# Both halves of the activations in one 512-column product, scaled and shifted ahead of it, and one adaLN vector from VectorE to TensorE

## The chip, the cores and the metric

The kernel runs on one core of one Trainium2 chip. The metric is device microseconds of one execution, weights and activations coming from HBM in float32 and the output going back to it. Three runs of the kernel before gave 672.47 us as their median (672.23 to 672.62).

## The reference

A trunk of two layers on a sequence of 256 tokens with 1024 channels. Layer 0 mixes tokens with a causal convolution module, layer 1 with causal attention of 16 heads; each mixer is followed by an MLP of 4096 hidden units with a squared ReLU. Six vectors per layer (shift, scale and gate of the mixer, then of the MLP) come from a conditioning vector `c` by a product with `ada_w`, called adaLN here.

```python
cond = silu(c)
for i in range(2):
    sh1, sc1, g1, sh2, sc2, g2 = split(cond @ ada_w[i] + ada_b[i], 6)
    h = rms_norm(x, mix_norm_g[i]) * (1 + sc1) + sh1
    y = conformer_conv(h, ...) if i == 0 else attention(h, w_qkv, q_norm_g, k_norm_g, w_o)
    x = x + g1 * y
    h = rms_norm(x, mlp_norm_g[i]) * (1 + sc2) + sh2
    x = x + g2 * (square(relu(h @ mlp_w1[i])) @ mlp_w2[i])
```

Everything is float32. The result must come out at nearly float32 accuracy.

## The kernel before

Activations lie transposed: 8 tiles (`KT`) of 128 channels by 256 tokens (`S`). `xT` holds the residual stream. A large product is done in float32r, a format with a shorter mantissa, and regains its accuracy by splitting: an operand is a high half plus a low half. For weights, `split` (lines 191 to 202) has ScalarE cast a loaded block `raw` of 128 x 2048 to the high half `wh` (L196), in two pieces of 1024 columns in the calls that matter here, and VectorE subtract to get the low half `wl` (L199; in layer 0 a quarter of it, 256 columns of each piece, goes to GpSimd, L201). For activations the halves are `xh` and `xl`, for the MLP's hidden values `sh` and `sl`, for attention's output `oh` and `ol`. `mm3` (lines 207 to 211) then makes one step of k, that is 128 input channels, out of three products: high weights on the high activations, high weights on the low ones, low weights on the high ones.

The normalization is put off. `norm_prep` (from L718) multiplies `xT` by the scale vector alone (`gm`) and splits it. The factor of each token, one over the root mean square, is not known yet when the first products start: `norm_scale` makes it during them, has it spread over the partitions as `rs_ext` (its copy there is called the seam), and `evict` (L796 and L797) multiplies each finished tile by it on VectorE. The shift vector rides along as two more columns of the activations, so these products have `NE` = 258 columns, and the bias that results stands in column 256 of the evicted tile and is added by the next operation on ScalarE.

An MLP (`mlp`, from L820) has two loops. **w1**: the 32 tiles `f` of 128 hidden units are made from 16 weight blocks of 256 units, two tiles a block, 8 steps of k a tile. `six` does the first three blocks in an order of its own, since the token factors come during them; the loop from L845 does blocks 3 to 15. Each tile goes through `finish` (L829 to 836): eviction (L797), Relu with its bias on ScalarE (L833), the square twice, once cast to the high half (L834, L835), and the low half by a subtraction on VectorE (L836). **w2**: from L868, four blocks of two output tiles, 32 steps of k each; a finished tile is scaled by the gate and added to `xT` by one VectorE operation (L881).

Attention makes q, k and v from twelve blocks of `w_qkv`, three for each `b` of 0 to 3 (q, k and v of four heads, `z` = 0, 1, 2; loop from L1049, `take` evicting with L797), and works on one group of heads while the products of the next run. Of that work the change touches `squares` (adds the biases to q and k, L951) and `values` (adds it to v); `norms` takes one over the root of the heads' mean squares with `rsqrt` (L175 to L180, eleven small VectorE operations, each waiting for the last) and widens it by a copy to `rb` (L971), which TensorE then transposes (`kb`, L991). `kouter` (from L763) is the output projection of both mixers.

TensorE's order is the order in which the code is written: `tick` counts steps of k, and `at(d, f)` puts `f` behind `d` more steps. The other engines' instructions are ordered by a scheduler, which weighs when their inputs should be ready. Loads are issued by SyncE in the order of its queue, into five buffers called `raw`.

adaLN vectors are made in two ways. `ada_dve` (L289) loads a quarter of a vector's weights (1 MB) and has VectorE multiply and add it in four pieces (L299, L301); after the last quarter `colsum` (L263) sums over partitions on TensorE (`cs`, L267) and two more small products turn the sum. `ada_pe` makes the same quarter with `gemv4` (L248): TensorE products on float32, each set of four side by side with 32 columns of weights. In the first MLP six vectors go the VectorE way: `slots` says after which block of w1 or w2 each quarter comes.

## Time and profile before

| | before |
|---|---|
| median of three runs | 672.47 us (672.23 to 672.62) |
| the profiled execution | 670.39 us |
| its span, first to last instruction | 668.6 us |
| TensorE products / weight loads, busy | 654.0 us / 605.2 us |
| VectorE, ScalarE, GpSimd, busy | 494.2, 369.2, 125.6 us |
| moved by DMA | 150.07 MB, 224 GB/s on average |
| conv layer | up to 155.98 us |
| first MLP, w1 and w2 | 155.98 to 253.5, 253.5 to 350.3 us |
| attention | 350.3 to 476.9 us |
| second MLP, w1 and w2 | 476.9 to 571.1, 571.1 to 664.1 us |

How to read it. PE is TensorE's products, PEld its weight loads, which overlap them; DVE is VectorE, ACT ScalarE, POOL GpSimd, SP SyncE. A product's length in a row is the time from its start to its modelled end, which overlaps the next, so the pace is read from the distance of starts, or from the number of products in a stretch. A row of windows has the stretch, its length, then for PE, PEld, DVE, ACT and POOL the busy time with the number of instructions in brackets, then TensorE's granted clock (1.00 is 2.4 GHz, 0.50 is 1.2 GHz), the busy share of the 16 DMA engines, and GB/s; where only one tile's or line's instructions are asked for, engines that have none are left out. A row of a timeline has the start, the length, engine, line, operation, output and inputs, sizes, the number of instructions put together, and in brackets the idle time before it with what ended it.

### The profile page before, as it was taken

What the parts mean: (1) busy time and instruction counts of PE and PEld (TensorE: products, weight loads), DVE (VectorE), ACT (ScalarE), POOL (GpSimd) and SP (SyncE); (2) the same over time, 40 slices, a digit from 0 to 9 for tenths busy, and PEclk for the clock granted to TensorE, in tenths of its full rate; (3) what the DMA queues carried; (4) which work ended last, traced back from release to release, by engine and by line L of the source; (5) the groups of instructions that cost most, each with busy time, mean ns of one, the idle gap of its engine ahead of it and who ended that gap; (6) DMA issues with size and microseconds to landing.
All of it is one profiled execution on the core that took longest, in us unless ns stands there. A gap on an engine that the chain in (4) does not pass through costs nothing.

```text
span 668.6 us, 14398 instructions
## 1 busy us (share of the span) xinstructions
PE 654.0 (98%) x5909; PEld 605.2 (91%) x5909; DVE 494.2 (74%) x924; ACT 369.2 (55%) x678; POOL 125.6 (19%) x167
## 2 busy tenths in 40 slices
...
GB/s 302 340 351 295 240 2 373 216 251 211 151 250 336 346 278 349 342 349 336 349 337 130 237 97 112 181 123 105 101 169 205 334 293 191 186 188 178 110 17 17
DMA packets 107871, 150.07 MB, mean 224 GB/s; under 512 B 2871, under 2 KB 91120, under 8 KB 107806
## 3 DMA queue, kind: packets, MB, share of 16 engines
...
q14 instruction: 19, 0.16, 0.1%
...
q10 hardware_dynamic: 144, 0.06, 0.0%
...
## 4 chain that ended last, share of the span: by engine, by line
PE 68%; DVE 21%; issue 4%; ACT 3%; POOL 2%; DMA 2%; SPq 1%; DVEq 0%; ACTq 0%; POOLq 0%
PE m L208 11%; PE m L210 11%; PE m L209 11%; DVE ada_a L301 8%; DVE wl L199 7%; PE qkv L208 4%; PE qkv L209 3%; PE qkv L210 3%; PE cv L403 3%; PE ko L209 2%; PE ko L208 2%; PE ci L208 2%; PE ko L210 2%; PE rep L393 2%; PE ci L210 2%
## 5 line engine op out<-in xcount | busy, mean ns | idle before, releaser
L199 DVE TENSOR_TENSOR wl<-raw,wh 128x1024 fp32r<-128x1024 f32 (+2 forms) x176 | 204.5, 1181 | 59.0 <-ACT wh L196 57.8
L196 ACT CAST wh<-raw 128x1024 fp32r<-128x1024 f32 x176 | 177.7, 1043 | 107.0 <-PE m L209 58.8
L210 PE MATMUL m<-xh,wl 128*128 128x258 f32 x512 | 144.5, 282 | 1.2 <-DVE wl L199 1.1
L208 PE MATMUL m<-sh,wh 128*128 128x256 f32 x512 | 145.4, 284 | 0.0
L210 PE MATMUL m<-sh,wl 128*128 128x256 f32 x512 | 144.3, 282 | 0.8 <-DVE wl L199 0.8
L208 PE MATMUL m<-xh,wh 128*128 128x258 f32 x512 | 145.1, 283 | 0.0
L209 PE MATMUL m<-xl,wh 128*128 128x258 f32 x512 | 144.7, 283 | 0.0
L209 PE MATMUL m<-sl,wh 128*128 128x256 f32 x512 | 144.0, 281 | 0.0
L210 PEld LDWEIGHTS m<-xh,wl 128*128 128x128 f32 x512 | 96.7, 189 | 1.8 <-DVE wl L199 1.8
L208 PEld LDWEIGHTS m<-sh,wh 128*128 128x128 f32 x512 | 96.4, 188 | 1.6 <-issue 0.8
L210 PEld LDWEIGHTS m<-sh,wl 128*128 128x128 f32 x512 | 96.4, 188 | 1.2 <-DVE wl L199 1.2
L208 PEld LDWEIGHTS m<-xh,wh 128*128 128x128 f32 x512 | 96.5, 188 | 1.0 <-issue 0.4
L209 PEld LDWEIGHTS m<-xl,wh 128*128 128x128 f32 x512 | 96.8, 189 | 0.0
L209 PEld LDWEIGHTS m<-sl,wh 128*128 128x128 f32 x512 | 96.4, 188 | 0.0
L201 POOL TENSOR_TENSOR wl<-raw,wh 128x256 fp32r<-128x256 f32 (+1 forms) x60 | 67.7, 1141 | 105.4 <-ACT wh L196 90.7
L301 DVE SCALAR_TENSOR_TENSOR ada_a<-raw,cond,ada_a 128x512 f32<-128x512 f32 x98 | 81.9, 867 | 0.9 <-DMA raw<-in_ada_w_dram 0.7
L208 PE MATMUL qkv<-xh,wh 128*128 128x258 f32 x192 | 56.4, 294 | 0.0
L209 PE MATMUL qkv<-xl,wh 128*128 128x258 f32 x192 | 54.2, 282 | 0.0
L210 PE MATMUL qkv<-xh,wl 128*128 128x258 f32 x192 | 54.1, 282 | 0.0
L833 ACT ACTIVATE s<-tx 128x256 f32<-128x256 f32 x64 | 31.8, 506 | 36.8 <-DVE tx L797 36.7
L730 POOL TENSOR_TENSOR acc<-acc,nsq 128x256 f32<-128x256 f32 x15 | 14.1, 937 | 155.4 <-ACT nsq L728 154.9
L208 PEld LDWEIGHTS qkv<-xh,wh 128*128 128x128 f32 x192 | 36.2, 189 | 4.2 <-issue 4.2
(256 smaller groups left out, 1125.2 us busy)
## 6 DMA issues: line engine op xcount, KB each, us to landing
...
```

The lines of the kernel that those rows point to most:

```text
L196: box["cut"] = [act.copy(wh[:, a:a + n], r[:, a:a + n]).ins]
L199: box["cut"].append(dve.tensor_sub(wl[:, a:m], r[:, a:m], wh[:, a:m].bitcast(F32)).ins)
L201: pool.tensor_tensor(wl[:, m:a + n], r[:, m:a + n], wh[:, m:a + n].bitcast(F32), op=OP.subtract)
L208: pe.matmul(ps, wh, ah, start=start, stop=False, **kw)
L209: pe.matmul(ps, wh, al, start=False, stop=False, **kw)
L210: pe.matmul(ps, wl, ah, start=False, stop=stop, **kw)
L301: dve.scalar_tensor_tensor(a, w, cond[:, k, 0:1], a, op0=OP.mult, op1=OP.add)
L393: pe.matmul(ps[32 * r:32 * r + 32, :284], ident[:, 32 * g:32 * g + 32], UT[i][:, r:r + 284], start=True, stop=True, tile_position=(0, 32 * ...
L403: pe.matmul(ps[32 * g:32 * g + 32, :S], W[:, g, q, :], G[:, g, 4 * q:4 * q + S], start=(q == 0), stop=(q == 7), tile_position=(0, 32 * g))
L730: pool.tensor_tensor(acc, acc, q, op=OP.add)
L833: act.activation(s, t[:, :S], AF.Relu, bias=t[:, S:S + 1])
```

## The change

Five things are changed. `xh` and `xl` become the two halves of one tile `X[0]` (named `xa`), beside each other for each k, and a second such tile `X[1]` (`xb`) is made after the conv layer. A new `mm2` does one step of k with two products where `mm3` has three: the high weights on both halves at once, 512 columns, into the two halves of one PSUM bank, and the low weights on the high half, 256 columns, into the first. It is used in w2 of both layers (512 steps), in blocks 5 to 15 of w1 of layer 1 (`MERGED`, 176 steps), and in seven of the twelve qkv blocks, from `b` = 1, `z` = 2 on (112 steps).

The bias columns fall away there: `whole` makes activations that are fully normalized, scaled and shifted: `xT` times `rs_ext` on VectorE, the same Identity with scale and bias twice on ScalarE (once cast to the high half), a subtraction on VectorE. It runs for the eight tiles at blocks 3 and 4 of w1 in both layers, into `xb`, and at `b` = 1, `z` = 0 and 1 of qkv, into `xa`. From block 5 on w1 reads `xb`. Layer 0 keeps `mm3` there, with 256 columns, and its Relu reads PSUM directly. Where `mm2` was used, the two halves of the bank are added: by `join` (a copy of one half on ScalarE, an addition on VectorE) in w1 and qkv, and in w2 by a second operation on `xT` like the first. In layer 1's shifted tiles VectorE makes the squared Relu, ScalarE the cast.

`su` now stores 24 of the 32 hidden tiles with both halves, the other eight go into `X[0]`, and `oh` and `ol` are the halves of `X[1]`. Tiles of q, k and v are used where they were evicted; only tiles that were not shifted still get their bias there.

The adaLN vector (1, 3), the shift of layer 1's MLP, leaves the first MLP, where VectorE made it in 16 pieces, and is made by TensorE at four qkv blocks (`ADA_AT`); the slots of the other five are spaced anew.

```diff
+MERGED = (1,)
+ADA_AT = ((1, 1), (1, 2), (2, 1), (2, 2))
...
+    def mm2(ps, wh, wl, a, start, stop):
+        pe.matmul(ps.rearrange("p (a s) -> p a s", a=2), wh, a, start=start, stop=False, skip_group_check=True)
+        pe.matmul(ps[:, :S], wl, a[:, 0, :], start=False, stop=stop, skip_group_check=True)
+        tick()
...
+    def whole(l, m, i, n):
+        t = work.tile([P, S], F32, name="nsq")
+        dve.tensor_mul(t, xT[:, i, :], rs_ext[:, :S])
+        g, b = gm[:, l, m, i:i + 1], mod[:, l, 3 * m, i:i + 1]
+        act.activation(X[n][:, i, 0, :S], t, AF.Identity, bias=b, scale=g)
+        act.activation(t, t, AF.Identity, bias=b, scale=g)
+        dve.tensor_sub(X[n][:, i, 1, :S], t, X[n][:, i, 0, :S].bitcast(F32))
+
+    def join(ps, t):
+        act.copy(t, ps[:, S:])
+        box["evict"] = dve.tensor_tensor(t, ps[:, :S], t, op=OP.add).ins
...
-            def finish(ps, f):
+            def both(f):
+                n = FF // P - KT
+                return su[:, f] if f < n else X[0][:, f - n, :, :S]
+
+            def finish(ps, f, shifted=False):
                 t = mp.tile([P, NE], F32, name="tx", bufs=3)
-                evict(ps, t)
                 s = mp.tile([P, S], F32, name="s2", bufs=4)
-                act.activation(s, t[:, :S], AF.Relu, bias=t[:, S:S + 1])
-                act.activation(sh[:, f, :], s, AF.Square)
-                act.activation(s, s, AF.Square)
-                dve.tensor_sub(sl[:, f, :], s, sh[:, f, :].bitcast(F32))
+                if shifted:
+                    if l in MERGED:
+                        join(ps, t[:, :S])
+                    if l not in MERGED:
+                        act.activation(s, ps[:, :S], AF.Relu)
+                    elif l == 0:
+                        act.activation(s, t[:, :S], AF.Relu)
+                    else:
+                        dve.scalar_tensor_tensor(s, t[:, :S], 0.0, t[:, :S], op0=OP.max, op1=OP.mult)
+                else:
+                    evict(ps, t)
+                    act.activation(s, t[:, :S], AF.Relu, bias=t[:, S:S + 1])
+                u = both(f)
+                if shifted and l == 1:
+                    act.copy(u[:, 0, :], s)
+                else:
+                    act.activation(u[:, 0, :], s, AF.Square)
+                    act.activation(s, s, AF.Square)
+                dve.tensor_sub(u[:, 1, :], s, u[:, 0, :].bitcast(F32))
...
             for b in range(3, FF // 256):
                 with tc.issue_after(box["seam"]) if b > 3 else ExitStack():
                     wh, wl = w1_split(b)
+                if b in (3, 4):
+                    for i in range(4 * b - 12, 4 * b - 8):
+                        whole(l, 1, i, 1)
+                if b == 5:
+                    use(1)
...
+                        if b > 4 and l in MERGED:
+                            mm2(ps, wh[:, o:o + P], wl[:, o:o + P], X[1][:, k, :, :S], k == 0, k == KT - 1)
+                        else:
+                            n = NE if b < 5 else S
+                            mm3(ps[:, :n], wh[:, o:o + P], wl[:, o:o + P], xh[:, k, :n], xl[:, k, :n],
+                                start=(k == 0), stop=(k == KT - 1))
+                    finish(ps, f, b > 4)
...
-                            mm3(ps[j][:, :S], wh[:, o:o + P], wl[:, o:o + P], sh[:, kk, :], sl[:, kk, :],
-                                start=(kk == 0), stop=(kk == FF // P - 1))
+                            mm2(ps[j], wh[:, o:o + P], wl[:, o:o + P], both(kk), kk == 0, kk == FF // P - 1)
...
-                        dve.scalar_tensor_tensor(xT[:, n, :], ps[j][:, :S], mod[:, l, 5, n:n + 1],
-                                                 xT[:, n, :], op0=OP.mult, op1=OP.add)
+                        for h in range(2):
+                            dve.scalar_tensor_tensor(xT[:, n, :], ps[j][:, h * S:h * S + S], mod[:, l, 5, n:n + 1],
+                                                     xT[:, n, :], op0=OP.mult, op1=OP.add)
...
-    seq = [[(0, 5), (1, 1)], [(1, 0), (1, 2), (1, 4), (1, 3)]]
+    seq = [[(0, 5), (1, 1)], [(1, 0), (1, 2), (1, 4)]]
...
-            slots[3 + n * 12 // len(fs) if half == 0 else 15 + n * 15 // len(fs)].append(f)
+            slots[5 + n * 9 // len(fs) if half == 0 else 14 + n * 16 // len(fs)].append(f)
...
+                if (b, z) in ADA_AT:
+                    kp = ADA_AT.index((b, z))
+                    r = ada_load(1, 3, kp)
+                    at(15, lambda kp=kp, r=r: fin3.append(ada_pe(1, 3, kp, r)))
+                    if kp == 3:
+                        at(20, lambda: fin3[3]())
...
+                if b == 1 and z < 2:
+                    for i in range(4 * z, 4 * z + 4):
+                        whole(1, 0, i, 0)
```

In the two qkv loops `mm3` and `evict` become `mm2` and `join` for the seven blocks named above (a tile made so counts as `shifted`).

How the order of instructions moves is shown at three places; in these rows a name's number tells one buffer from another, and a line number is that of the kernel the row is from. The first is ScalarE in w1 of layer 0, around the cast of block 5's weights. Before (`wh_2405` is block 5; `s2_2279` and `s2_2311` are tiles 6 and 7):

```order
L835 ACTIVATE s2_2230<-s2_2230 128x256
L835 ACTIVATE s2_2237<-s2_2237 128x256
L833 ACTIVATE s2_2279<-tx_2277 128x256
L196 CAST wh_2405<-raw_2403 128x1024
L834 ACTIVATE sh_1997<-s2_2279 128x256
L833 ACTIVATE s2_2311<-tx_2309 128x256
L835 ACTIVATE s2_2279<-s2_2279 128x256
L834 ACTIVATE sh_1997<-s2_2311 128x256
L196 CAST wh_2405<-raw_2403 128x1024
```

After (`wh_2434` is block 5; `xb_1995` and the `nsq` tiles belong to `whole`, `s2_2394` and `s2_2426` to tiles 8 and 9):

```order
L815 ACTIVATE xb_1995<-nsq_2358,mod_142,gm_143 128x256
L876 ACTIVATE s2_2394<-tx_2393 128x256
L816 ACTIVATE nsq_2358<-nsq_2358,mod_142,gm_143 128x256
L815 ACTIVATE xb_1995<-nsq_2363,mod_142,gm_143 128x256
L881 ACTIVATE su_2000<-s2_2394 128x256
L816 ACTIVATE nsq_2363<-nsq_2363,mod_142,gm_143 128x256
L882 ACTIVATE s2_2394<-s2_2394 128x256
L876 ACTIVATE s2_2426<-tx_2425 128x256
L202 CAST wh_2434<-raw_2432 128x1024
L881 ACTIVATE su_2000<-s2_2426 128x256
L202 CAST wh_2434<-raw_2432 128x1024
```

Between the last operation of tiles 0 to 5 and that cast now stand 26 operations instead of one: 16 of `whole` and 10 of `finish` for tiles 6 to 9. In layer 1 there are 28.

The second place is VectorE at the same point, up to the low half of block 5. Before (`wl_2406` is that low half, `tx_2309` tile 7's eviction, `ada_a` the accumulation of an adaLN quarter):

```order
L797 TENSOR_TENSOR tx_2309<-m1_2284,rs_ext_142 128x258
L299 TENSOR_SCALAR ada_a_2318<-raw_2316,cond_104 128x512 x2
L301 SCALAR_TENSOR_TENSOR ada_a_2318<-raw_2316,cond_104,ada_a_2318 128x512
L836 TENSOR_TENSOR sl_1998<-s2_2279,sh_1997 128x256
L301 SCALAR_TENSOR_TENSOR ada_a_2318<-raw_2316,cond_104,ada_a_2318 128x512
L199 TENSOR_TENSOR wl_2406<-raw_2403,wh_2405 128x768
L836 TENSOR_TENSOR sl_1998<-s2_2311,sh_1997 128x256
L797 TENSOR_TENSOR tx_2358<-m1_2333,rs_ext_142 128x258
L199 TENSOR_TENSOR wl_2406<-raw_2403,wh_2405 128x768
```

After (`wl_2435` is that low half, `tx_2425` tile 9's eviction, the subtractions into `xb` and the `nsq` product are of `whole`, the one into `su` is tile 8's):

```order
L824 TENSOR_TENSOR tx_2425<-m1_2400,rs_ext_140 128x258
L311 TENSOR_SCALAR ada_a_2506<-raw_2504,cond_104 128x512 x2
L817 TENSOR_TENSOR xb_1995<-nsq_2348,xb_1995 128x256
L817 TENSOR_TENSOR xb_1995<-nsq_2353,xb_1995 128x256
L813 TENSOR_TENSOR nsq_2363<-xT_137,rs_ext_140 128x256
L313 SCALAR_TENSOR_TENSOR ada_a_2506<-raw_2504,cond_104,ada_a_2506 128x512 x2
L817 TENSOR_TENSOR xb_1995<-nsq_2358,xb_1995 128x256
L313 SCALAR_TENSOR_TENSOR ada_a_2506<-raw_2583,cond_104,ada_a_2506 128x512
L817 TENSOR_TENSOR xb_1995<-nsq_2363,xb_1995 128x256
L883 TENSOR_TENSOR su_2000<-s2_2394,su_2000 128x256
L313 SCALAR_TENSOR_TENSOR ada_a_2506<-raw_2583,cond_104,ada_a_2506 128x512 x2
L205 TENSOR_TENSOR wl_2435<-raw_2432,wh_2434 128x768 x2
```

The low half now comes behind the eviction of tile 9, seven pieces of adaLN and six short operations, where it came behind tile 7's.

The third place is VectorE in attention, where `norms` of the first group of heads ends in `rb`. Before:

```order
L179 SCALAR_TENSOR_TENSOR rsq_t_4727<-rsq_t_4727,vs_4724 128x16
L951 TENSOR_SCALAR q_4894<-tqkv_4757 128x256
L180 SCALAR_TENSOR_TENSOR rsq_y_4726<-rsq_t_4727,rsq_y_4726 128x16
L178 TENSOR_TENSOR rsq_t_4727<-rsq_y_4726 128x16
L199 TENSOR_TENSOR wl_4979<-raw_4976,wh_4978 128x1024
L179 SCALAR_TENSOR_TENSOR rsq_t_4727<-rsq_t_4727,vs_4724 128x16
L199 TENSOR_TENSOR wl_4979<-raw_4976,wh_4978 128x1024
L180 SCALAR_TENSOR_TENSOR rsq_y_4726<-rsq_t_4727,rsq_y_4726 128x16
L797 TENSOR_TENSOR tqkv_4792<-qkv_4767,rs_ext_142 128x258
L971 COPY rb_4740<-rsq_y_4726 128x512
L974 TENSOR_TENSOR ws_4742<-vs_4724,rsq_y_4726 128x8
```

After (`tk_4564` is an eviction of the second group; L1011 adds a bias; `xa` and `nsq` are of `whole`):

```order
L185 SCALAR_TENSOR_TENSOR rsq_t_4477<-rsq_t_4477,vs_4474 128x16
L817 TENSOR_TENSOR xa_138<-nsq_4524,xa_138 128x256
L186 SCALAR_TENSOR_TENSOR rsq_y_4476<-rsq_t_4477,rsq_y_4476 128x16
L824 TENSOR_TENSOR tk_4564<-qkv_4539,rs_ext_140 128x258
L184 TENSOR_TENSOR rsq_t_4477<-rsq_y_4476 128x16
L1011 TENSOR_SCALAR tq_4456<-tq_4456 128x256
L185 SCALAR_TENSOR_TENSOR rsq_t_4477<-rsq_t_4477,vs_4474 128x16
L1011 TENSOR_SCALAR tq_4507<-tq_4507 128x256
L186 SCALAR_TENSOR_TENSOR rsq_y_4476<-rsq_t_4477,rsq_y_4476 128x16
L817 TENSOR_TENSOR xa_138<-nsq_4529,xa_138 128x256
L1031 COPY rb_4490<-rsq_y_4476 128x512
L1034 TENSOR_TENSOR ws_4492<-vs_4474,rsq_y_4476 128x8
```

Between `vs`, with which `norms` begins, and `rb` now stand eight short operations of `whole` and one piece of a weight block's low half, where two such pieces stood.

## Rows read from the trace of the kernel before

**Rows 1.** Engines (page, part 1): busy us (share of the span) and instructions
```profile
PE 654.0 (98%) x5909; PEld 605.2 (91%) x5909; DVE 494.2 (74%) x924; ACT 369.2 (55%) x678; POOL 125.6 (19%) x167
```

**Rows 2.** Stages (windows): w1, w2 of layer 0; attention; w1 of layer 1
```profile
156.00:253.50 97.50, 96.30 (x805) 94.40 (x803) 90.29 (x152) 67.23 (x127) 31.10 (x32) 1.00 0.78 260
253.50:350.30 96.80, 95.97 (x816) 93.78 (x814) 91.93 (x118) 44.05 (x64) 41.01 (x35) 1.00 1.02 345
350.30:476.90 126.60, 125.24 (x1043) 114.00 (x1043) 100.91 (x278) 75.70 (x165) 3.43 (x23) 1.00 0.45 144
476.90:571.10 94.20, 94.20 (x793) 93.66 (x793) 75.38 (x130) 70.42 (x134) 2.10 (x3) 1.00 0.66 216
```

**Rows 3.** Waits of TensorE: us in total, times, longest
```profile
PE m L210 <- DVE wl L199: 1.8, 3, 0.8
```

**Rows 4.** Windows of the products alone: w1, then w2, of layer 1
```profile
510.10:561.70 51.60, 51.60 (x434) 51.60 (x433) 7.55 (x18) 0.00 (x0) 1.00 0.87 288
577.20:594.30 17.10, 17.10 (x146) 17.10 (x145) 0.48 (x1) 0.00 (x0) 1.00 0.56 181
```

**Rows 5.** Timeline of TensorE, an adaLN product in the conv stage: start, us
```profile
106.73 1.91 PE L248 MATMUL ada<-raw,cond 128*32 128x256 f32 x32
108.46 0.40 PE L403 MATMUL cv<-xg,W 128*32 128x256 f32 x4
```

**Rows 6.** Timeline of TensorE, a column sum
```profile
350.26 0.64 PE L267 MATMUL cs<-ada_a,ones 128*32 128x256 f32 x8
```

**Rows 7.** Timeline of ScalarE, first tiles of w1 in layer 0, then layer 1
```profile
174.36 0.91 ACT L833 ACTIVATE s<-tx 128x256 f32<-128x256 f32 x2 [2.04 <-DVE tx L797]
180.47 0.50 ACT L833 ACTIVATE s<-tx 128x256 f32<-128x256 f32 x1
180.87 1.04 ACT L196 CAST wh<-raw 128x1024 fp32r<-128x1024 f32 x1
...
495.03 0.91 ACT L833 ACTIVATE s<-tx 128x256 f32<-128x256 f32 x2 [1.95 <-DVE tx L797]
501.13 0.50 ACT L833 ACTIVATE s<-tx 128x256 f32<-128x256 f32 x1
```

**Rows 8.** Line 443: durations min/median/max in ns, first and last start
```profile
L443 ACT ACTIVATE h<-xg,mod,gm x8: 583/592/602, 45.4 to 59.5; 128x256 f32<-128x256 f32 x8
```

**Rows 9.** Timeline of VectorE, w1 of layer 0
```profile
173.91 1.82 DVE L797 TENSOR_TENSOR tx<-m,rs_ext 128x258 f32<-128x258 f32 x5
175.65 0.95 DVE L199 TENSOR_TENSOR wl<-raw,wh 128x768 fp32r<-128x768 f32 x1
...
189.50 1.40 DVE L301 SCALAR_TENSOR_TENSOR ada_a<-raw,cond,ada_a 128x512 f32<-128x512 f32 x2
190.82 0.41 DVE L836 TENSOR_TENSOR sl<-s,sh 128x256 fp32r<-128x256 f32 x1
```

**Rows 10.** Windows of the w1 products alone, up to block 5, layers 0, 1
```profile
155.90:186.40 30.50, 29.33 (x240) 28.89 (x241) 3.48 (x9) 0.00 (x0) 1.00 0.45 145
476.90:507.20 30.30, 29.14 (x240) 28.87 (x241) 3.52 (x9) 0.00 (x0) 1.00 0.35 108
```

**Rows 11.** Windows at the program's end; timeline of TensorE at its start
```profile
665.20:667.20 2.00, 0.00 (x0) 0.00 (x0) 0.00 (x0) 0.37 (x1) 0.00 (x0) 1.00 0.43 131
667.30:668.50 1.20, 0.00 (x0) 0.00 (x0) 0.00 (x0) 0.00 (x0) 0.00 (x0) 0.50 0.00 0
...
2.63 3.78 PE L117 MATMUL wu<-ident 128*128 128x128 f32 x16
12.81 1.60 PE L117 MATMUL wu<-ident 128*128 128x128 f32 x12
```

**Rows 12.** Timelines of VectorE and of TensorE in attention
```profile
381.10 0.41 DVE L971 COPY rb<-rsq_y 128x512 f32<-128x512 f32 x1
...
382.06 0.60 PE L991 MATMUL kb<-ident,rb 128*128 128x128 f32 x4
```

**Rows 13.** Timeline of VectorE at the program's end
```profile
664.18 0.48 DVE L881 SCALAR_TENSOR_TENSOR xT<-m,mod,xT 128x256 f32<-128x256 f32 x1 [2.36 <-PE m L210]
```

60 lines of the change are left out of this document (38 added, 22 removed).

## The prediction

> **What bounds the kernel now.** The busy share comes first: TensorE is busy for 98% of the span [rows 1]. In the view of the stages it stays so in both MLPs and in attention, and the only other thing that is full anywhere is in the first MLP, where VectorE is busy for 90.29 of 97.5 us in w1 and 91.93 of 96.8 us in w2, with the DMA engines at 1.02 in w2 [rows 2]. The view of waits asks whether these hold TensorE up: hardly, for in both MLPs it waited only three times, 1.8 us in all, for the low half of a weight [rows 3]. So the time is the pace of TensorE's products, and that pace is the next thing to read: 144 products of w2 of the second MLP in 17.1 us, and 432 of its w1 in 51.6 us (the counts shown have two more that reach over an edge) [rows 4]. That is 119 ns each, 356 and 358 ns for the three that make one step of k; qkv has w1's 258 columns, and I give it w1's pace.
>
> **The product of 512 columns.** A step was three products of 256 columns and becomes one of 512 and one of 256. This holds for 512 steps of w2 (256 per layer), 176 of w1 (blocks 5 to 15 of layer 1) and 112 of qkv (seven of twelve weight blocks): 800 steps. No row shows a float32r product of 512 columns. The nearest is adaLN's float32 product: eight sets of four side by side took 1.73 us from 106.73 to 108.46 [rows 5], 216 ns a set, where a set of 256 float32 columns keeps the array nearly twice as long as 256 float32r columns do. The bounds around it: a step stays at 356 ns if 512 columns cost twice 119, and it falls to 216 + 108 = 324 ns if the 256-column product too ran at half of that set. Between them stands the case that the 12 ns by which 119 exceeds 256 columns at 2.4 GHz (106.7 ns; the granted clock is 1.00 [rows 4]) are paid once per product: 225 + 119 = 344 ns. I take 216 + 119 = 335 ns: the long product by the row that is nearest to it, the short one at today's pace, because the weights behind it are still loaded under only 256 columns. Gain: 512 x 21 + 176 x 23 + 112 x 23 ns = 10.8 + 4.1 + 2.6 = 17.5 us, all of it on the path, since TensorE is the path. At 344 ns it is 10.3 us, at 356 ns 0.7, at 324 ns 26.3.
>
> **What else TensorE gains.** Layer 0's 176 steps of w1 lose the two bias columns: 176 x 2.3 ns = 0.4 us. VectorE loses 22 evictions and 16 accumulations of the moved vector in the first MLP, so the short waits on wl go: 1.8 us [rows 3], with the restart of each about 2.5 us; at worst they stay. One column sum of four products goes, 0.6 us [rows 6].
>
> **The moved vector.** In attention TensorE gets four visits of two four-fold products, 64 pieces (a float32 product shows as two): 64 / 32 x 1.73 = 3.5 us [rows 5], and about 0.2 us of changing over at each visit, as the column sum shows, whose eight pieces take 0.64 us and not 0.43 [rows 5, 6]: 4.3 us, on the path. Its four loads go behind qkv loads on SP's queue, where the DMA share is 0.45 [rows 2]: nothing. In the first MLP 4 MB less are loaded; w2 then needs 16 + 12 MB, at 345 GB/s [rows 2] 85 us, under TensorE's time there, so DMA binds nothing.
>
> **The new wait at block 5 of w1.** From block 5 on TensorE reads activations that are already scaled and shifted. `whole` makes them on VectorE and ScalarE, eight tiles of two operations on each. The order shows where this stands: ahead of the cast of block 5's weights on ScalarE, and its last pieces, with seven pieces of adaLN, ahead of block 5's low half on VectorE. Before, that cast came right behind the first operation of tile 6. In layer 0 ScalarE's work for tiles 0 to 5 ran from 174.36 to 180.47, 1.02 us a tile; the Relu alone took 0.40 [rows 7]. Ahead of the cast now stand tiles 6 to 8 whole (3.1), tile 9's Relu (0.4), and 16 operations of `whole`. The nearest row to these is L443, the same Identity with a scale and a bias from memory, 592 ns of duration [rows 8]; an operation of 0.50 us starts its successor after 0.40 [rows 7], so 0.49 each, 7.8 us. 180.47 + 11.3 + 0.95 for the first half of the cast = 192.7. VectorE, which must evict tile 9 after TensorE is through with it, then has seven pieces of adaLN (five of 0.66, two of some 0.4) and six short operations of 0.35, 6.2 us in all, before it gets to the low half (0.95) [rows 9]: 186.5 + 0.35 + 6.2 + 0.95, with a little for what it waits on ScalarE, 194.2. TensorE ended its 240 products of tiles 0 to 9 at 186.5 [rows 10], and would need that low half 0.24 us later: a wait of 7.5 us where there was none. Layer 1 has no adaLN there but the whole of tile 9 ahead of the cast: 501.13 [rows 7] + 7.8 + 4.1 + 0.95 + 1.2 for the low half = 515.2, against 507.5: 7.7 us. With 0.40 per `whole` operation each wait is 1.4 us shorter; more than 8.5 us is not in the queues.
>
> **TensorE's clock.** Such a wait has no like in the MLPs, where the longest was 0.8 us [rows 3]. At the program's end TensorE had no work from 665.2 on, and the granted clock went from 1.00 to 0.50 between 667.2 and 667.3 [rows 11], from 2.4 to 1.2 GHz. What the lower level costs is seen at the start, where TensorE came from rest: 16 products of 128 columns took 3.78 us, 236 ns each, and from 12.81 on twelve of the same took 1.60 us, 133 ns each [rows 11]. So I expect about half pace behind each wait: it costs nothing if the clock holds, and at most half of the 10.2 us that lie between those two rows, 5.1 us. I take 1.8 us each, an estimate near the lower third, since the program's start also waits for loads: 3.6 us together.
>
> **Attention and the end.** `whole` runs once more beside qkv's second block: 16 operations of 0.35 us on VectorE, 15 of them ahead of `rb` in its order, 5.2 us. `rb` was ready 0.6 us ahead of its transposes [rows 12]. Two thirds I let fall into the gaps between the eleven small operations of `rsqrt`, each of which waits for the last; 1.7 us stays, and TensorE waits 1.1 us (0 to 4.6). Block 2's low half stands ahead of `whole` there, so no wait of the other kind. At the end a second accumulation of the last tile follows the first, 0.4 us [rows 13].
>
> **Sum.** -17.5 - 0.4 - 2.5 - 0.6 + 4.3 + 7.5 + 7.7 + 3.6 + 1.1 + 0.4 = +3.6 us. The profiled execution took 670.39 us (its span 668.6), so 674.0 by its own time; the median of the runs, 672.47, is 2.1 us above it: 676.1.
>
> **Rivals.** *The wait comes, the clock holds*: 3.6 us less, 672.5, no change. For it: the clock is 1.00 in every stage [rows 2], behind waits of 0.8 us too. Against it: the end of the trace. *The overhead is per product*, 344 ns a step: 7.2 us more, 683.3. For it: 119 ns differs by 1 ns between 256 and 258 columns, as columns at 2.4 GHz would, so the rest looks fixed. Against it: 216 ns for the long float32 sets, with loads of 32 columns though. *The product does not do what it says*, 356 ns: 692.9. Against it the same row. *The loads vanish altogether*, 324 ns a step on all 800: 8.8 us better than my sum, 667.3, faster; it decides as soon as a step falls under 331 ns, where the sum is zero. For it: with half as many reloads per column the array need never wait for one. Against it: today's 119 ns, with each load under a 256-column product, which the second half of every step still is. The Trainium skill, TensorE: Matmul & The Clock Gate, section Back-to-back issue gap, gives columns over 2.4 GHz plus 2.5 ns, 216 and 109 ns, which is this rival; the trace disagrees for 256 columns, 119 ns. *ScalarE's queue is done in time*: were `whole` hidden, both waits and the clock's loss go, 657.3. Against it: both of layer 0's queues are full, and even at 0.40 us for each operation of `whole` the cast's first half ends at 191.3, 4.8 us late.
>
> **How the numbers follow.** The sum as it stands 0.36 (674 to 680, the attention's bound within); clock holding 0.13, no change; overhead per product 0.20; no gain from 512 columns 0.05; loads vanishing 0.16; waits hidden 0.10. Faster 0.26, the last two; same, within 0.2%, which is about what a measurement of this kernel can tell from no change, 0.13; slower 0.61. The range leaves out no gain (0.05) and hidden waits (0.10): 667 to 684.
>
> **What would show it.** Right: products of 512 columns 216 ns apart from the next one and 119 behind it, a wait of 7 to 8 us on wh and wl at the first product of block 5 in both layers' w1, a granted clock under 1.00 in the stretch behind it, no wait on wl in the first MLP afterwards. Wrong: a step of 344 or 324 ns; block 5 starting without a wait, or behind one under 3 us; TensorE waiting in w1 of layer 1 on the longer eviction.

## The result: 693.7 us, 3.3% slower, and by more than any case of the prediction's range

The changed kernel took 693.72 us (median of five runs, 693.18 to 694.49), the kernel before 672.23 us beside it. The ratio is 1.033 (95% interval 1.031 to 1.0349). The forecast was 676.1 us with a range of 667 to 684: the direction was right, the size was not, and the time lies almost on the rival that had been given 0.05 and left out of the range, that the product of 512 columns brings nothing (692.9 us). That agreement is luck: the product did bring something, and other terms cost more than forecast (the last part shows both).

The profiled execution took 693.18 us with a span of 691.4, 22.8 us more than before. Read from the first product of each stage, in us:

| stage | before | after | difference |
|---|---|---|---|
| conv layer | 155.98 | 158.37 | +2.4 |
| w1, layer 0 | 97.52 | 107.60 | +10.1 |
| w2, layer 0 | 97.34 | 93.33 | -4.0 |
| attention, from the first qkv product | 92.57 | 98.14 | +5.6 |
| output projection of attention | 33.56 | 34.98 | +1.4 |
| w1, layer 1 | 94.13 | 102.50 | +8.4 |
| w2, layer 1, to the end | 97.47 | 96.49 | -1.0 |

### The profile page after: what moved, and what is told of

Read it like the earlier page. It is cut to its first block, busy times and chain, and to the rows that moved or that the text cites. A ratio compares the mean times of both kernels' runs of the same rounds, so it can differ in the third digit from the quotient of the medians.

```text
span 691.4 us, 12958 instructions
## 1 busy us (share of the span) xinstructions
PE 658.2 (95%) x5165; PEld 570.4 (82%) x5165; DVE 505.6 (73%) x964; ACT 379.4 (55%) x712; POOL 136.6 (20%) x167
## 4 chain that ended last, share of the span: by engine, by line
PE 82%; ACT 7%; DVE 4%; POOL 2%; DMA 1%; issue 1%; SPq 1%; DVEq 0%; ACTq 0%; POOLq 0%
PE m L221 23%; PE m L222 12%; PE m L214 5%; PE m L216 5%; PE m L215 4%; PE qkv L221 3%; PE cv L415 3%; PE ci L214 2%; PE ko L214 2%; PE ko L215 2%; PE ko L216 2%; PE rep L405 2%; PE ada L260 2%; PE ci L216 2%; PE ci L215 2%; DMA keep<-in_conv_w_in_dram 1%
## 5 line engine op out<-in xcount | busy, mean ns | idle before, releaser
L221 PE MATMUL m<-su,wh 128*128 128x512 f32 x384 | 136.2, 398 | 0.0
L222 PE MATMUL m<-su,wl 128*128 128x256 f32 x384 | 107.2, 279 | 0.0
L221 PEld LDWEIGHTS m<-su,wh 128*128 128x128 f32 x384 | 72.1, 188 | 17.5 <-issue 0.8
L222 PEld LDWEIGHTS m<-su,wl 128*128 128x128 f32 x384 | 72.4, 188 | 0.0
L221 PE MATMUL m<-xb,wh 128*128 128x512 f32 x176 | 63.6, 404 | 6.9 <-ACT wh L202 6.9
L214 PE MATMUL m<-xb,wh 128*128 128x256 f32 x176 | 51.1, 290 | 6.2 <-ACT wh L202 6.2
L216 PE MATMUL m<-xb,wl 128*128 128x256 f32 x176 | 51.3, 292 | 2.1 <-POOL wl L207 1.2
L215 PE MATMUL m<-xb,wh 128*128 128x256 f32 x176 | 50.9, 289 | 0.0
L222 PE MATMUL m<-xb,wl 128*128 128x256 f32 x176 | 50.4, 286 | 0.5 <-DVE wl L205 0.5
L221 PEld LDWEIGHTS m<-xb,wh 128*128 128x128 f32 x176 | 34.3, 195 | 15.2 <-ACT wh L202 7.1
L214 PE MATMUL m<-xa,wh 128*128 128x258 f32 x160 | 45.6, 285 | 0.0
L215 PE MATMUL m<-xa,wh 128*128 128x258 f32 x160 | 45.5, 284 | 0.0
L221 PE MATMUL m<-xa,wh 128*128 128x512 f32 x128 | 45.4, 396 | 0.0
L742 POOL TENSOR_TENSOR acc<-acc,nsq 128x256 f32<-128x256 f32 x15 | 12.5, 834 | 158.9 <-ACT nsq L740 158.4
L221 PE MATMUL qkv<-xa,wh 128*128 128x512 f32 x112 | 42.1, 412 | 0.0
L214 PEld LDWEIGHTS m<-xb,wh 128*128 128x128 f32 x176 | 34.9, 198 | 7.3 <-ACT wh L202 6.4
```

The source lines that it names most:

```text
L214: pe.matmul(ps, wh, ah, start=start, stop=False, **kw)
L215: pe.matmul(ps, wh, al, start=False, stop=False, **kw)
L216: pe.matmul(ps, wl, ah, start=False, stop=stop, **kw)
L221: pe.matmul(ps.rearrange("p (a s) -> p a s", a=2), wh, a, start=start, stop=False, skip_group_check=True)
L222: pe.matmul(ps[:, :S], wl, a[:, 0, :], start=False, stop=stop, skip_group_check=True)
```

## The profile after

TensorE has 744 instructions fewer than in [rows 1] and is busy for 4 us more, and its share has fallen from 98% to 95% (the page's first part, then the four stages of [rows 2] as windows):

```profile
PE 658.2 (95%) x5165; PEld 570.4 (82%) x5165; DVE 505.6 (73%) x964; ACT 379.4 (55%) x712; POOL 136.6 (20%) x167
```

```profile
158.40:265.90 107.50, 99.14 (x804) 97.07 (x803) 97.36 (x157) 76.50 (x152) 41.09 (x34) 0.95 0.77 262
266.00:359.20 93.20, 93.20 (x550) 79.83 (x549) 77.23 (x95) 39.45 (x53) 43.71 (x53) 1.00 0.87 289
359.30:492.30 133.00, 129.02 (x992) 109.34 (x990) 103.42 (x289) 84.70 (x189) 1.69 (x3) 1.00 0.50 162
492.40:594.80 102.40, 95.05 (x615) 85.97 (x614) 88.02 (x168) 67.27 (x129) 2.08 (x3) 0.95 0.60 200
```

Both w1 stages now hold some 7 to 8 us in which TensorE had nothing to do, and a granted clock under 1.00; w2 of layer 0 has neither. The waits of TensorE name the place; [rows 3] had 1.8 us in three for both MLPs:

```profile
PE m L221 <- ACT wh L202: 6.9, 1, 6.9
PE m L214 <- ACT wh L202: 6.2, 1, 6.2
...
PE m L216 <- POOL wl L207: 1.2, 1, 1.2
PE ko L788 <- DVE tv L821: 1.2, 1, 1.2
...
PE kb L1052 <- DVE rb L1031: 1.0, 1, 1.0
...
PE m L216 <- DVE wl L205: 0.9, 1, 0.9
```

The first two are the first product of block 5 of w1, in layer 1 and in layer 0, where it waits for the high half of its weights. The timeline of ScalarE at that place in layer 0 (L815 and L816 are `whole`, L876 is tile 9's Relu) shows why, as the order did:

```profile
192.76 0.41 ACT L881 ACTIVATE su<-s 128x256 fp32r<-128x256 f32 x1
193.07 0.59 ACT L816 ACTIVATE nsq<-nsq,mod,gm 128x256 f32<-128x256 f32 x1
193.56 0.41 ACT L882 ACTIVATE s<-s 128x256 f32<-128x256 f32 x1
193.87 0.50 ACT L876 ACTIVATE s<-tx 128x256 f32<-128x256 f32 x1
194.27 1.03 ACT L202 CAST wh<-raw 128x1024 fp32r<-128x1024 f32 x1
```

No operation there waited for anything; the cast simply came last. TensorE had started its last product of block 4 at 188.83 and started block 5 at 195.35. Windows around it, with the columns of [rows 2]:

```profile
189.00:193.00 4.00, 0.11 (x1) 0.00 (x0) 3.95 (x10) 4.00 (x10) 0.00 (x0) 1.00 0.00 0
193.00:195.00 2.00, 0.00 (x0) 0.00 (x0) 2.00 (x6) 2.00 (x5) 0.00 (x0) 0.72 0.46 84
195.00:204.00 9.00, 6.53 (x27) 5.94 (x28) 8.85 (x10) 5.92 (x9) 8.62 (x4) 0.50 0.37 127
204.20:206.00 1.80, 1.80 (x17) 1.80 (x17) 0.95 (x2) 0.78 (x2) 1.80 (x3) 1.00 1.05 374
```

The granted clock fell to 0.50, which is 1.2 GHz, while TensorE stood still, stayed there for 10 us (one more short wait falls into them), and the 27 products behind the wait came 213 ns apart instead of 119 wherever nothing else held them.

The other thing to read is the pace of the new product, in w2 of layer 1 (timeline of TensorE: start, length, line L221 with 512 columns, L222 with 256):

```profile
624.93 0.28 PE L222 MATMUL m<-su,wl 128*128 128x256 f32 x1
625.05 0.40 PE L221 MATMUL m<-su,wh 128*128 128x512 f32 x1
625.29 0.28 PE L222 MATMUL m<-su,wl 128*128 128x256 f32 x1
625.41 0.40 PE L221 MATMUL m<-su,wh 128*128 128x512 f32 x1
```

The long product holds the array for 0.24 us, the short one for 0.12. Over the 226 uninterrupted steps of that stage a step takes 350.0 ns, where 227 steps before took 355.9; in w1 of layer 1 it is about 348.5 against 358.4, in qkv 351.4 against 359.8. So 800 steps give back 512 x 5.9 + 176 x 9.9 + 112 x 8.4 = 5.7 us, not 17.5.

## Experiments

Times of whole runs are medians beside the kernel before on the same chip (671.3 to 671.9 us there). The table has the stages of each profiled span; conv is listed apart, because it varies from run to run whatever the kernel (experiment 8).

| | conv | w1, 0 | w2, 0 | qkv | out | w1, 1 | w2, 1 | sum without conv |
|---|---|---|---|---|---|---|---|---|
| before | 155.98 | 97.52 | 97.34 | 92.57 | 33.56 | 94.13 | 97.47 | 512.6 |
| after | 158.37 | 107.60 | 93.33 | 98.14 | 34.98 | 102.50 | 96.49 | 533.0 |
| 1, w2 alone | 159.10 | 97.71 | 98.10 | 92.57 | 33.56 | 94.13 | 96.84 | 512.9 |
| 3, late use | 155.81 | 106.45 | 93.33 | 98.17 | 34.96 | 102.46 | 96.50 | 531.9 |
| 4, spread | 159.74 | 103.62 | 93.33 | 98.18 | 34.97 | 96.39 | 96.50 | 523.0 |
| 5, filled wait | 158.66 | 107.55 | 93.33 | 98.18 | 34.99 | 100.66 | 96.50 | 531.2 |
| 6, vector back | 158.02 | 108.57 | 95.40 | 97.74 | 34.99 | 102.32 | 96.50 | 535.5 |
| 7, qkv as before | 160.04 | 107.61 | 93.33 | 101.14 | 33.48 | 101.84 | 96.50 | 533.9 |
| 9, no scaled activations | 158.82 | 100.85 | 93.53 | 97.37 | 33.54 | 94.13 | 96.84 | 516.3 |
| 10, and old slots | 158.72 | 97.54 | 93.64 | 97.32 | 33.56 | 94.13 | 96.84 | 513.0 |
| 8, filled conv wait | 156.55 | 97.54 | 96.12 | 92.61 | 33.56 | 94.13 | 96.85 | 510.8 |
| 11, vector on VectorE in attention | 156.39 | 97.60 | 93.64 | 98.34 | 33.56 | 94.13 | 96.85 | 514.1 |

### 1. The 512-column product alone

Into the kernel before goes only this, with what it needs (the hidden halves beside each other, the second addition to `xT`):

```diff
-                            mm3(ps[j][:, :S], wh[:, o:o + P], wl[:, o:o + P], sh[:, kk, :], sl[:, kk, :], ...)
+                            mm2(ps[j], wh[:, o:o + P], wl[:, o:o + P], su[:, kk], kk == 0, kk == FF // P - 1)
```

> The kernel before with one part of the change: the 512 steps of w2 as one product of 512 columns and one of 256 (hidden halves beside each other, second addition to the residual); w1, attention and all adaLN vectors as before. Theory A, a float32r product costs about 0.45 ns for each column and only some 5 ns for itself (233 and 117 ns in the changed kernel, 119 before): a step goes from 356 to about 350 ns, 512 x 6 = 3 us less, less 0.4 us at the end, so about 669 us against 672. Theory B, which the prediction used, long products shed 21 ns a step and something else in the changed kernel (other engines' traffic, the waits) hid it: 10.8 us less, about 661 us. Neither expects a new wait of TensorE in w1.

672.77 us against 671.87, ratio 1.0011 (0.9993 to 1.003): no difference. In layer 1 w2 and the end took 0.6 us less (1.5 by the step, less what the second addition costs at the end). In layer 0 it took 0.8 us more, since TensorE now waits for VectorE:

```profile
PE m L216 <- DVE wl L199: 2.0, 3, 1.1
```

VectorE was busy for 93.67 of 98.10 us there. Theory A's step holds (351 ns in both layers), and its 3 us do not come in: while all six vectors are made in the first MLP, VectorE sets w2's pace in layer 0.

### 2. The disputed price by itself

Two kernels put series of 48 products (for the pairs, 32 of them) behind w2 of layer 1, when every other engine is through. The core of it:

```diff
+                        pe.matmul(ps[:, :m], wt[:, o:o + P], sh[...][:, :m], start=True, stop=True)
```

> The kernel before with six series of products put behind w2 of layer 1, where DMA, VectorE and ScalarE have nothing left to do, each with alternating weights: 48 float32r products of 256 columns (pa), 48 of 512 (pb), 48 of 128 (pc), 32 pairs of 512 and 256 (pd), 48 of 512 columns of zeros (pe), 48 of 512 bfloat16 columns (pf); about 50 us in all. Theory A, the price is per column and lies in TensorE's own pace: pa 118 to 119 ns, pb 230 to 234, pc about 61, pd 350 a pair. Theory B, other engines' traffic slows long products: pa 119, pb 216 to 219, pd 335. If the operands' values matter (power), pe is nearer to 216 than pb; if the width of float32r matters, pf is.

> The kernel before with six series of 48 products behind w2 of layer 1, alternating weights: float32r with 512 columns (qa) and 256 columns (qb) on weights of only 32 columns, float32r with 384 (qc) and 192 columns (qd) on full weights, bfloat16 with 256 (qe) and 128 columns (qf). Theory A, float32r data is taken in at some 0.445 ns a column, whatever the weights: qa 232, qb 118 to 119, qc 175.6, qd at its weight load's time (111 ns) or above; bfloat16 at 0.417 ns a column, qe 109. Theory B, the load of full float32r weights slows the product that it runs beside: qa 216, qb 109, and qc 170 or less.

Mean distance of starts, from the first and the last start of each series:

| columns | float32r, weights 128 x 128 | float32r, weights 128 x 32 | bfloat16, weights 128 x 128 |
|---|---|---|---|
| 128 | 110.6 ns | | 55.8 ns |
| 192 | 111.3 | | |
| 256 | 118.7 | 113.7 | 109.4 |
| 384 | 175.4 | | |
| 512 | 232.5 (zeros: 234.2) | 230.6 | 216.1 |

Timelines of TensorE in the two kernels (pb: float32r, 512 columns; pf: bfloat16, 512, four in a row; qa: float32r, 512, weights of 32 columns):

```profile
674.02 0.39 PE L905 MATMUL pb<-sh,wl 128*128 128x512 f32 x1
674.26 0.39 PE L905 MATMUL pb<-sh,wh 128*128 128x512 f32 x1
674.49 0.39 PE L905 MATMUL pb<-sh,wl 128*128 128x512 f32 x1
...
709.68 1.03 PE L913 MATMUL pf<-h 128*128 128x512 bf16 x4
```

```profile
669.97 0.40 PE L919 MATMUL qa<-sh,wl 128*32 128x512 f32 x1
670.21 0.40 PE L919 MATMUL qa<-sh,wh 128*32 128x512 f32 x1
```

The 32 pairs of 512 and 256 columns took 353 ns a pair. For long products this is theory A in both kernels. From 256 to 512 columns float32r takes (232.5 - 118.7) / 256 = 0.445 ns a column and about 5 ns for the product; 384 columns lie on that line (0.445 x 384 + 5 = 175.7, measured 175.4). Other engines' traffic has no part in it, nor do the values. The load of full weights has 2 to 5 ns: on weights of 32 columns 256 columns took 113.7 ns, halfway between the two theories, but the price of a column did not fall, (230.6 - 113.7) / 256 = 0.457 ns. The same array takes bfloat16 at (216.1 - 109.4) / 256 = 0.417 ns a column, which is 2.4 GHz. The Trainium skill, TensorE: Matmul & The Clock Gate, section Back-to-back issue gap, gives columns over 2.4 GHz plus 2.5 ns: bfloat16 agrees here (109.2 and 215.8 ns by it, 109.4 and 216.1 measured), float32r does not. With 128 and with 192 columns a float32r product on full weights takes 111 ns alike; theory A had expected 61 for 128. Only the first two products of these series started 59 and 89 ns apart, near the line's 62 and 90, and the weight loads then start 0.1 us apart: they may be what holds the rest back, which was not tested by itself.

### 3. Reading the new activations later

```diff
-                if b == 5:
+                if b == 8:
                     use(1)
```

(with the limits on `b` for bias columns and `mm2` moved alike).

> The changed kernel, but w1 reads the scaled and shifted activations from block 8 on instead of block 5 (blocks 5 to 7 keep the bias columns and the eviction); the scaled activations are made at the same place, and on ScalarE block 5's cast still stands behind their 16 operations. Theory A, TensorE waits because the cast and the split of block 5's weights are late in ScalarE's and VectorE's queues: the waits at block 5 stay in both layers, 5 to 7 us each, and with them the half clock, so about 692 us. Theory B, TensorE waits for the scaled activations themselves: no wait at block 5, the half clock does not come, about 675 us.

689.46 us in one run, 4.3 under the median of the changed kernel, of which 2.6 are the conv stage's. Both waits stayed, though block 5 read nothing new:

```profile
PE m L214 <- ACT wh L202: 13.8, 2, 6.9
```

Theory A: TensorE waits for weights that stand behind `whole` in ScalarE's queue, not for what `whole` makes.

### 4. Spreading the work

On top of that, `whole` runs two tiles a block in blocks 4 to 7.

```diff
-                if b in (3, 4):
-                    for i in range(4 * b - 12, 4 * b - 8):
+                if b in (4, 5, 6, 7):
+                    for i in range(2 * b - 8, 2 * b - 6):
```

> The changed kernel, w1 reading the scaled and shifted activations from block 8 on, and these made two tiles a block in blocks 4 to 7, so that on ScalarE only four of the 16 operations stand ahead of block 5's cast. Theory A, it was the order of ScalarE's queue: both waits of 6 to 7 us go, the clock stays at 1.00 in both w1, and the 21 us that waits and slow products took in w1 of the two layers come back but for about 1 us: 673 us or a little less. Theory B, ScalarE and VectorE have no room for this work in w1 at all, and the wait only comes back in pieces at blocks 6 to 9, 3 us or more a layer: 680 us or more.

683.64 us, ratio 1.0175 (1.0154 to 1.0197) to the kernel before, 10 us less than the changed kernel. Both theories were half right. In layer 1 w1 fell to 96.39 us and the waits at blocks 5 are gone (one of 1.3 us stayed, later). In layer 0 w1 fell only to 103.62, because a wait of 4.6 us came for a low half at block 7, on VectorE, and the granted clock was 0.50 from 205.3 to 212 us behind it:

```profile
PE m L216 <- DVE wl L205: 5.2, 3, 4.6
...
PE m L222 <- DVE wl L205: 1.3, 1, 1.3
```

### 5. Filling the wait

```diff
                 if b == 5:
+                    wm = held("wm")
+                    for _ in range(50 if l == 0 else 56):
+                        pe.matmul(wm[:, :S], X[0][:, 0, 0, :P], X[0][:, 0, 0, :S], start=True, stop=True)
                     use(1)
```

> The changed kernel with 50 (layer 0) and 56 (layer 1) float32r products of 256 columns ahead of block 5's first product, written to a bank that nobody reads: they fill the wait of TensorE without shortening it. Theory A, the products behind the wait run at half clock because TensorE stood still: the granted clock stays at 1.00, the first products of block 5 are 119 ns apart and not 213, and some 2.5 us a layer come back, about 689 us. Theory B, the clock falls there for another reason (the load on the chip): the time stays at 693 to 694 us and the clock falls all the same.

691.43 us, ratio 1.0289 (1.0264 to 1.0315), 2 us less than the changed kernel. In layer 1 it went as theory A has it: w1 took 1.8 us less and the clock stayed at 1.00 through the wait and behind it. In layer 0 the clock held too, but TensorE, now faster, ran into the next thing that was late, the low half on GpSimd (2.2 us) behind the late cast, stood still again, and the clock fell then. Windows, first layer 1, then layer 0:

```profile
523.00:529.60 6.60, 6.60 (x57) 6.60 (x57) 3.70 (x10) 6.60 (x16) 0.00 (x0) 1.00 0.00 0
...
531.00:535.00 4.00, 3.61 (x20) 3.17 (x21) 4.00 (x5) 4.00 (x6) 0.00 (x0) 1.00 0.35 79
```

```profile
189.00:195.00 6.00, 6.00 (x52) 6.00 (x51) 5.88 (x14) 6.00 (x15) 0.00 (x0) 1.00 0.11 16
195.00:200.80 5.80, 2.24 (x15) 1.62 (x13) 5.80 (x9) 5.04 (x7) 5.08 (x2) 1.00 0.46 169
201.00:204.00 3.00, 3.00 (x16) 3.00 (x17) 1.77 (x2) 0.24 (x1) 3.00 (x3) 0.54 0.23 56
```

So in layer 1 it was TensorE's standing still that took the clock down. Layer 0 won nothing by the filling (107.55 against 107.60 us): the low half of that second wait came 42.2 us after the start of w1 in both kernels, so half a clock ahead of it had cost nothing, and behind it the clock was low in both.

### 6. The vector back on VectorE

```diff
-ADA_AT = ((1, 1), (1, 2), (2, 1), (2, 2))
+ADA_AT = ()
```

(and (1, 3) back in the list of vectors of the first MLP).

> The changed kernel with the one adaLN vector back on VectorE in the first MLP, none of it in attention. Theory A, VectorE is what bounds w2 of layer 0 once steps are shorter: TensorE saves 4.3 us in attention (about 98.1 to 94 us from the first qkv product to the output projection), and w2 of layer 0 goes from 93.3 to 97 or 98 us, as it was where w2 alone was merged: no change within 1 us, 693 us. Theory B, VectorE hides the vector there: w2 of layer 0 grows by one column sum (0.9 us) alone, 690 us.

695.08 us, ratio 1.0343 (1.0321 to 1.0364): no gain, as theory A has it, but not for its reasons alone. w2 of layer 0 grew by 2.1 us. In attention the 4.4 us of TensorE's work went, yet the stage lost only 0.4: in its place stand waits, the longest one on `ws`, where 0.5 us stood before, and about 1 us by the half clock behind it.

```profile
PE kb L1052 <- DVE ws L1034: 3.1, 2, 2.8
```

```profile
414.30:417.50 3.20, 2.79 (x10) 2.52 (x11) 1.50 (x6) 1.19 (x2) 0.00 (x0) 0.50 0.72 276
```

### 7. Attention's products as before

```diff
             def merged():
-                return (b, z) >= (1, 2)
+                return False
```

(and no `whole` for qkv). Here qkv and attention's output share `xb`, so later qkv blocks read activations over which the output has been written: values differ, the instructions do not, but two waits of 0.9 and 0.7 us on those writes come with it.

> The changed kernel with attention's products as before: three products a step, bias columns, no scaled and shifted activations for qkv; the adaLN vector stays in attention. Theory A, at 8 ns a step the 512-column product brought 0.9 us to qkv and the scaled activations cost more, by the waits on rb (1.0 us) and on ws (0.5) that were not there before: the stretch from the first qkv product to the output projection falls from 98.1 us by 0.5 to 1.5 us. Theory B, the waits have nothing to do with it and come from the adaLN products: the stretch grows by 0.9 us.

The qkv stretch took 101.14 us, 3.0 more than in the changed kernel. Some 1.7 us of that are the two waits of the edit's own, and behind them the granted clock was 0.50, so that twelve qkv products took 2.7 us where 1.4 is usual:

```profile
438.00:441.30 3.30, 3.30 (x17) 3.30 (x17) 1.78 (x11) 0.20 (x1) 0.00 (x0) 0.50 0.94 303
```

The edit's own cost is thus as large as the whole difference, the waits on `rb` and `ws` (1.5 us) were gone, and this run decides nothing on the qkv stretch. Experiments 9 and 10 do, which have attention's products as before, with the vector on TensorE, and no such waits: 97.37 and 97.32 us, 0.8 less than in the changed kernel, as theory A has it. The output projection was 1.5 us shorter, 33.48 and so as before: its wait of 1.2 us on `tv`, the sum in `join`, came with that step. The bank of the last v tile is wanted by the projection and comes free only when ScalarE and VectorE have both had it.

### 8. Filling the wait in the conv stage

The change does not touch the conv stage, and it took 155.8 to 160.0 us. The rows that part are TensorE's wait for a small adaLN product (timeline) and the clock behind it (window), first in the changed kernel, then in the kernel before:

```profile
20.23 0.37 PE L253 MATMUL adac<-ones,ada_s 128*128 128x1 f32 x1 [2.20 <-ACT ada_s L248]
```

```profile
19.90:26.50 6.60, 6.27 (x29) 6.27 (x30) 4.37 (x12) 1.19 (x4) 1.76 (x1) 0.50 1.07 364
```

```profile
20.55 0.27 PE L241 MATMUL adac<-ones,ada_s 128*128 128x1 f32 x1 [0.98 <-ACT ada_s L236]
```

```profile
20.60:26.50 5.90, 5.90 (x56) 5.50 (x59) 4.00 (x12) 0.91 (x2) 1.58 (x1) 1.00 1.08 367
```

All twelve traces without the filling below agree: the stage took 155.8 to 156.0 us where the clock held (three), 157.4 and 158.0 where it was low for about 3 us, 158.4 to 160.0 where it was low for about 7 (seven). The length of the wait alone does not decide: in experiment 6 the clock fell behind 1.66 us, and in the first kernel of experiment 2 it held behind 2.02, with a stage of 155.87 us:

```profile
20.36 0.61 PE L241 MATMUL adac<-ones,ada_s 128*128 128x1 f32 x4 [2.02 <-ACT ada_s L236]
```

```profile
20.50:26.50 6.00, 6.00 (x59) 5.42 (x59) 3.93 (x12) 0.91 (x2) 1.76 (x1) 1.00 1.07 366
```

The kernel below is the one before, with w2 of layer 1 in 512-column products and:

```diff
         def go():
+            if q == 1:
+                hold = aux("wu")
+                for _ in range(12):
+                    pe.matmul(hold[:, :S], xh[:, 0, :P], xh[:, 0, :S], start=True, stop=True)
             fin()
```

> The kernel before with w2 of layer 1 alone in 512-column products (0.6 us less there by the run in which w2 alone was merged), and 12 float32r products of 256 columns on data at hand, written to a bank that nobody reads, ahead of the small adaLN product in the conv stage for which TensorE waits 1 to 2.5 us at 18 to 20 us of the span. Theory A, the runs of one kernel differ by up to 4 us because in some of them this wait is long and the clock then falls to half for some 6 us: with the wait filled the conv stage takes 155.5 to 156.5 us in every run, the granted clock is 0.999 or more, and the median is about 669.5 us, 2 us under that of the kernel before. Theory B, the spread comes from elsewhere (the loads' arrival): times spread from 670 to 674 us as before.

670.08 us (12 runs, 669.0 to 671.2) against 671.74 (17 runs, 669.9 to 673.6), ratio 0.9976 (0.9963 to 0.9988): a quarter of a per cent faster than the kernel before, and the only version here that beats both. No run had a mean clock under 0.998, where runs of the kernel before had down to 0.995, and its slowest ones the lowest. In the profiled run w2 of layer 0 was 1.2 us shorter too, without the two waits of before, so not all of the 1.7 us is the filling's. Six of the 17 runs of the kernel before had a mean clock of 0.999 or more; their median is 670.7 us, so that about 1.0 us of the 1.7 goes with the clock. The runs still spread over 2.2 us. The wait that stayed is short:

```profile
18.30 1.59 PE L484 MATMUL wu<-xh 128*128 128x256 f32 x12
20.39 0.61 PE L246 MATMUL adac<-ones,ada_s 128*128 128x1 f32 x4 [0.50 <-ACT ada_s L241]
```

### 9 and 10. Without the scaled activations

The changed kernel's w2 and its vector on TensorE, and nothing else; in 10 also with the old spacing of the adaLN quarters:

```diff
-            slots[5 + n * 9 // len(fs) if half == 0 else 14 + n * 16 // len(fs)].append(f)
+            slots[3 + n * 12 // len(fs) if half == 0 else 15 + n * 15 // len(fs)].append(f)
```

> The changed kernel without its scaled and shifted activations: w2 of both layers in products of 512 and 256 columns and the one adaLN vector on TensorE in attention, with the slots of the change; w1 and qkv as before, with bias columns and three products a step. Theory A, all that the change lost beyond 5 us comes from making those activations (the waits in w1, the half clock behind them, the waits on rb): w1 takes 97.5 and 94.1 us, w2 of layer 0 some 93.3, the stretch from the first qkv product to the output projection 92.6 + 4.4 = 97.0 us, and the time is within 1 us of the kernel before. Theory B, TensorE's work for the vector or the new slots cost more than 5 us by themselves: 676 us or more.

> The run without scaled and shifted activations (w2 in 512-column products, vector on TensorE in attention), but with the slots of the adaLN quarters as the kernel before spaced them. In that run w1 of layer 0 took 100.9 us with one wait of 3.1 us on a low half, where the kernel before takes 97.5. Theory A, the new spacing puts adaLN pieces ahead of a weight block's low half on VectorE: with the old spacing w1 of layer 0 takes 97.5 to 98 us, and the span less the conv stage is 513 us or less. Theory B, the wait comes from the 512-column form or the missing vector: 100 us or more again.

9 took 676.50 us, ratio 1.0072 (1.0051 to 1.0093), and 10 took 673.61 in one run (its conv stage 2.7 us longer than in the profile of before). Without conv the sums are 516.3 and 513.0 us, against 512.6 before and 533.0 after. So making the scaled activations, with what follows from it, costs 17 us with the slots alike, and 20 against the old slots. The new slots alone cost 3.3, by a wait that the old ones do not have, and the half clock behind it (0.50 from 211.6 to 214.9 us):

```profile
PE m L211 <- DVE wl L200: 3.1, 1, 3.1
```

In VectorE's timeline of 9 that low half stands behind four pieces of adaLN, the first three of them 2.06 us:

```profile
204.82 2.06 DVE L307 SCALAR_TENSOR_TENSOR ada_a<-raw,cond,ada_a 128x512 f32<-128x512 f32 x3
206.80 0.41 DVE L803 TENSOR_TENSOR tx<-m,rs_ext 128x258 f32<-128x258 f32 x1
207.18 0.74 DVE L841 TENSOR_TENSOR su<-s,su 128x256 fp32r<-128x256 f32 x1
207.84 0.74 DVE L307 SCALAR_TENSOR_TENSOR ada_a<-raw,cond,ada_a 128x512 f32<-128x512 f32 x1
208.50 2.34 DVE L200 TENSOR_TENSOR wl<-raw,wh 128x768 fp32r<-128x768 f32 x2
```

The vector's move is a trade and no gain. Against experiment 1, which has the same w2 and the vector in the first MLP, w2 of layer 0 falls by 4.5 us in experiment 10 and attention grows by 4.8; the sums are 512.9 and 513.0.

### 11. The vector on VectorE, in attention

```diff
-                    at(15, lambda kp=kp, r=r: fin3.append(ada_pe(1, 3, kp, r)))
+                    ada_dve(1, 3, ADA_AT.index((b, z)))
```

(with the old slots, w2 of both layers in 512-column products, and experiment 8's filling).

> The kernel before with w2 of both layers in products of 512 and 256 columns, the old spacing of slots, the conv stage's wait filled with 12 products, and the one adaLN vector made by VectorE beside attention's products at the same four qkv blocks, not by TensorE. Theory A, VectorE has room in attention (100.9 us busy of 126.6 before): w1 97.5, w2 of layer 0 93.5 to 94, the qkv stretch 92.6 to 93.5, w1 and w2 of layer 1 94.1 and 96.8, conv 156 to 157; about 668 us as a median, 3 to 4 us under the kernel before. Theory B, the 16 pieces fall in front of rb or a low half on VectorE, and TensorE waits there for 3 us or more: 671 us or more.

670.75 us, ratio 0.9988 (0.9975 to 1.0002): not told apart from the kernel before. Theory B: the qkv stretch took 98.34 us, 5.8 more, with waits where they were feared:

```profile
PE kb L1000 <- DVE rb L980: 2.2, 1, 2.2
PE kb L1000 <- DVE ws L983: 1.0, 1, 1.0
```

Behind the first the clock fell too, as the window from 380 us shows:

```profile
380.00:384.00 4.00, 2.96 (x16) 2.96 (x17) 3.55 (x9) 1.09 (x2) 0.00 (x0) 0.68 1.09 367
```

VectorE's mean share of 80% in attention [rows 2] says nothing of the chain that ends in `rb`.

## Why the prediction was wrong, term by term

| term (us) | predicted | measured | from |
|---|---|---|---|
| 800 steps with 512 columns | -17.5 | -5.7 | step lengths, above; experiments 1, 2 |
| two bias columns fewer in layer 0 | -0.4 | 0.0 | mean distance of starts, 119.5 ns with 256 columns as with 258 |
| waits on low halves gone | -2.5 | -3.4 | gaps of TensorE's starts before: 2.0 in w1, 1.4 in w2 of layer 0, with restarts |
| one column sum gone | -0.6 | -0.7 | the same |
| vector on TensorE | +4.3 | +4.8 | experiments 9, 10; its 64 pieces take 4.0 us, the small products 0.4 |
| wait at block 5, layer 0 | +7.5 | 6.4, and 3.0 behind it | gaps of TensorE's starts |
| wait at block 5, layer 1 | +7.7 | 7.1, and 1.0 behind it | the same |
| clock behind both | +3.6 | 4.5 | 27 products, and 7 steps, at half pace |
| wait on `rb` | +1.1 | +1.3 | starts of `kb` |
| bank of the last qkv tile | none | +1.2 | wait on `tv`; experiment 7 |
| end, second addition | +0.4 | +0.6 | wait of `ot`, 1.0 against 0.4 |
| conv stage | none | +2.4 | clock at 20 to 26 us; experiment 8 |

The measured column adds up to 22.5 of the 22.8 us between the two profiled executions.

**The step that failed** is "216 + 119 = 335 ns". It took the long product from the row nearest in length [rows 5], a float32 set, and that row is of another format: float32r is taken in at 0.445 ns a column, not 0.417, and the long product took 232.5 ns instead of 216. The rival of an overhead per product was wrong as well. It split 119 ns into 106.7 for columns and 12 for the product, by the 1 ns between 256 and 258 columns; but one nanosecond cannot tell 0.445 from 0.417 ns a column, and by the line of experiment 2 about 7 of the 12 ns belong to the columns. The measured step of 350 ns lies halfway between that rival's 344 and the 356 of the one with 0.05, that the product does not do what it says. The latter's total comes nearest only because 5.0 us more of gain than it had meet 5.8 us more of cost elsewhere. The one with 0.05 should have had far more, since no row showed a float32r product of another length, and its price (twice 119) was the only end taken from the same format. 11.8 us of the 17.6 between forecast and result are this term.

**What held.** The waits at block 5 were read from the order of the queues and the durations of single rows and came out within 2 us each: the cast's first half was forecast to end at 192.7 and ended at 195.3, of which 2.4 us are the stage's later start. What was missing is what stands behind the late cast, the low half on GpSimd (1.2 us) and on VectorE (0.9 us), each with its restart. The rival that ScalarE is done in time fell by the waits themselves, and the reading that TensorE waits for the activations by experiment 3. The clock fell during both waits and cost 4.5 us, within the bound of 5.1 each; experiment 5 showed that only layer 1's share of it was to be had by filling. About half of what the waits cost lay in the place of `whole` and not in its amount: against experiment 3, which has the same operations, experiment 4 took 8.9 us away outside the conv stage.

**What was not seen.** That evicting the last qkv tile takes two engines and holds a bank that the output projection needs (1.2 us); and that the conv stage, which the change does not touch, differs between two profiles by as much as a small term. The 2.1 us between the profiled execution and the median of before, which the prediction added without a reason, are most likely this: the runs with the lower mean clock are the longer ones.

**What stays open.** Of the 5.6 us in the qkv stretch experiments 9 and 10 put 4.8 on the vector's products; the 0.8 that are left, the waits on `rb` and `ws` less the gain of the shorter steps, were not taken apart, since experiment 7 made waits of its own and experiment 6 shows that the adaLN products and the wait on `ws` cover each other. Why float32r is taken in at 0.445 ns a column was not found; only values, traffic and the width of the weights are ruled out, and the bfloat16 series changed the format of both operands at once.
